# Latent heads' values as seven half-block products, and one VectorE operation on attention scores

## The chip, the cores and the metric

The kernel runs on one core of one Trainium2 chip. The metric is the device time of one execution in microseconds. Three runs of the kernel before gave 896.74, 900.17 and 900.93 us; their median is 900.17 us. An execution taken by the profiler is one more run.

## The reference

One hybrid decoder layer on 512 tokens of width 2048, in float32. Cut to what the change touches:

```python
q = (_rms_norm(q_lat, g_q) @ w_uq).reshape(b, s, 8, 192)        # 128 + 64 rotary
kv = (_rms_norm(kv_lat, g_kv) @ w_ukv).reshape(b, s, 8, 256)    # per head: 128 key, 128 value
k_nope, v = kv[..., :128], kv[..., 128:]
# latent heads: scores = (q_nope k_nope + q_rope k_rope) * 192**-0.5
# forgetting heads: scores = q k * 128**-0.5 + c[q] - c[k],  c = cumsum(log_sigmoid(f))
p = softmax(where(key <= query, scores, -inf)); o = p @ v
```

There are eight latent heads and eight forgetting heads of width 128. Their outputs, each times a SiLU gate, go through `w_out`, a norm and the residual.

## The kernel before

All large products keep float32 accuracy on TensorE by splitting each operand into a rounded part and a rest (`hi`, `lo`) and adding three matmuls (`mm3`, L148 to L151). Weights come in chunks of up to 128 x 1024. `load` (L231) starts a chunk's DMA on SP, `divide` (L269) makes `whi` with a ScalarE copy (L276) and `wlo` with a VectorE subtraction (L279). `chunk` (L289) loads four chunks ahead and divides two ahead. The raw chunks of the latent stage share three buffers.

Four of the large projections (forgetting values `v`, latents `l`, latent gates `m`, output `o`) are not multiplied plainly. They are cut in two by two half blocks and computed with seven products in place of eight, named p1, p2, p4, q6, g7, g5 and g3. `operand_steps` (L880) makes the sums of the left operand on VectorE. The sums of weight blocks (`t7`, `t6`, `t4`, `t5`) are made in DRAM by `sum_blocks` (L316): a DMA copy from SP (L312) and an accumulating DMA from POOL (L309) for each, one step at a time, paced by `paced` (L532) against the matmul loops; a step of 1 MB (the `o` sums) takes twice the pace.

The order is: forgetting heads' values, queries, keys and gates in pairs of heads (to about 460 us of the profile), latents and latent gates (to about 586 us), the latent heads in four pairs (to about 718 us), the output projection. Attention steps wait in a queue, `todo`; `pump` runs a few of them after each slice of a projection, so that their matmuls lie between those of the projection. The program order of each engine is set by a scheduler, which may move an instruction ahead of others that aren't ready in its own model.

In the latent stage each pair of heads runs a query projection (L1505: six slices of nine 512-wide matmuls), the rotary turn of the queries (L865, L870, L1514), then one loop over four slices of `w_ukv` (L1533 to L1549) that makes keys (two outputs, six 512-wide matmuls a slice) and values (four token blocks, twelve 256-wide matmuls a slice, named `mv`). PSUM has four banks for projections (`pj`), three for attention (`at`) and one for the output of a head.

`Head.scores` (L616) does, for each block of 128 queries: the score matmuls (L628); on VectorE for a latent head the mask on the diagonal block (L630) and the row maximum (L643), for a forgetting head one or two additions of `c` (L636, L639) and the maximum; on ScalarE the exponential (L650); on VectorE the reciprocal (L651) and the scaling (L652). The score bank is held until the exponential has read it. `forget_cols` (L784) turns `c` into columns with four transposes (L787); `load_keys` and `forget_keys` (L790, L795) bring `-c` rows with and without the mask. `rotary_key` (L1103) turns the shared rotary key early in the kernel.

Of the kernel before, what the change touches and what calls it, by code (L numbers as in the profile page):

```python
# [19 lines left out]
P = 128  # L20
D = 2048
S = 512
# [22 lines left out]
KL = L4 + ROPE  # L45
NSLOT = 28
# [19 lines left out]
def tile_hybrid_layer(  # L66
# [105 lines left out]
    gains2 = cst.tile([P, P], F32, name="gains2")  # L172
    pool.memset(gains2, 0.0)
# [22 lines left out]
    mask = cst.tile([P, P], F32, name="mask")  # L196
# [21 lines left out]
    raws, ready = {}, {}  # L218
# [12 lines left out]
    def load(i, small=None):  # L231
# [3 lines left out]
        if cols is None:  # L235

            raw = raw_tile(i)
            to = raw if len(w.shape) == 2 else raw.rearrange("p (k c) -> p k c", k=2)
            nc.sync.dma_start(to, w)
# [76 lines left out]
    def sum_blocks(g, block, late, width=512):  # L316

        n = 2 * width
        for name in ("t7", "t6", "t4", "t5"):

            W[name, g] = [dr.tile([P, n + 16], F32, name=f"{name}{g}{j}")[:, :n] for j in range(4)]
        for j in range(4):
# [11 lines left out]
    def add_products(names, plain):  # L334
# [3 lines left out]
        for name, g in names:  # L338
# [3 lines left out]
            else:  # L342
                for j in range(4):
                    w = W[sums[name], g][j]
                    w, second = w if isinstance(w, tuple) else (w, None)
                    of = g if g in AT else "o"
# [14 lines left out]
    for g in "vlm":  # L361
        sum_blocks(g, lambda j, h, c, g=g: in_block(g, j, h, c), ("t4", "t5"))

# [21 lines left out]
    mla = []  # L385
    for p in range(4):
        mla.append(
            {
                "q": add_chunks(
                    w_uq,  # L390
                    [
                        (0, 2 * QK * p, NOPE),
                        (NOPE, 2 * QK * p + QK, NOPE),
                        (2 * NOPE, 2 * QK * p + NOPE, ROPE),
                        (2 * NOPE + ROPE, 2 * QK * p + QK + NOPE, ROPE),
                    ],
                    QR // P, 2, 2 * QK,
                ),
                "kv": add_chunks(w_ukv, [(0, 512 * p, 512)], KVR // P, 2, 512),
            }  # L400
        )
# [141 lines left out]
    def proj_T(rng, outs, kh, kl, rate=1):  # L543
# [3 lines left out]
        for i in rng:  # L547
            hi, lo = chunk(i)
# [59 lines left out]
    class Head:  # L608
# [7 lines left out]
        def scores(self, b):  # L616
# [7 lines left out]
            else:  # L624
                for kind, (qh, ql), (kh, kl) in zip(("nope", "rope"), self.q, self.k):
                    pairs += [(qh, kh), (qh, kl), (ql, kh)] if kind == "nope" else [(qh, kh), (ql, kh)]
# [1164 lines left out]
```

## Time and profile before

| | |
|---|---|
| Median of three runs | 900.17 us (896.74 to 900.93) |
| The profiled execution, its own time | 897.76 us |
| Its span, first to last instruction | 896.0 us |
| TensorE busy | 883.9 us, 99% of the span |
| VectorE busy | 678.7 us, 76% |
| ScalarE busy | 453.8 us, 51% |
| Mean granted TensorE clock | 0.997 of 2.4 GHz |

The profile is one execution. A busy time is the union of an engine's instructions; matmuls overlap, and their ends are modelled, so the time a matmul costs is read from the distance between starts. A queue such as SP or POOL issues DMAs in order.

### The profile page before, as it was taken

To read this page: it belongs to the slowest core of one execution; us is meant where nothing else is said; L and a number is where in the kernel's file an instruction comes from. 1 tells how busy PE (TensorE), PEld (TensorE's weight loads), DVE (VectorE), ACT (ScalarE), POOL (GpSimd) and SP (SyncE) were. 2 spreads that over 40 slices of the span, in tenths; PEclk is the share of its full clock that TensorE was granted. 3 is DMA by queue.
4 is the path that set the end of the run, shared out by engine and by line. 5 is a ranking of instruction groups with operands and counts; after the bars stand their busy time and mean duration, and the time that the engine had idled before them with its cause. 6 is when DMAs were issued, how large, how long until landed. Compare 5 with 4: busy or idle time off the path is not lost.

```text
span 896.0 us, 12851 instructions
## 1 busy us (share of the span) xinstructions
PE 883.9 (99%) x4598; PEld 755.2 (84%) x4598; DVE 678.7 (76%) x1123; ACT 453.8 (51%) x837; POOL 65.7 (7%) x86
## 2 busy tenths in 40 slices
PE   9999999999999999999999999999999999999996
PEld 8988887888888888888998998788888888888885
DVE  4579995648766838577588898967877995988785
ACT  6944443334344323335445565535555676646383
POOL 1010110011211101000000000000000000000021
PEclk9999999999999999999999999999999999999998
DMA  9798799789899999996899984799762137799878
GB/s 294 235 265 250 215 322 298 233 237 305 242 278 274 245 235 254 243 267 154 275 395 393 342 297 138 159 235 233 190 147 91 51 118 219 239 325 312 269 217 250
DMA packets 125659, 218.26 MB, mean 244 GB/s; under 512 B 16378, under 2 KB 54036, under 8 KB 124572
## 3 DMA queue, kind: packets, MB, share of 16 engines
q1 hardware_dynamic: 113484, 179.47, 61.2%
q0 software_dynamic: 11376, 37.75, 20.7%
q8 instruction: 36, 0.59, 0.3%
q10 hardware_dynamic: 736, 0.22, 0.1%
q14 instruction: 27, 0.22, 0.1%
HBM read 202.72 MB, written 65.03 MB: 299 GB/s over the span
## 4 chain that ended last, share of the span: by engine, by line
PE 85%; DVE 8%; DMA 3%; ACT 2%; issue 1%; SPq 0%; DVEq 0%; ACTq 0%
PE fk L149 3%; PE fk L151 3%; PE fq L149 3%; PE fk L150 3%; PE fq L151 3%; PE fq L150 3%; PE in L585 3%; PE sm L628 2%; DVE wlo L279 2%; PE fg L149 2%; PE fg L150 2%; PE fg L151 2%; PE oa L149 2%; PE oa L151 2%; PE oa L150 2%; PE mq L149 2%
## 5 line engine op out<-in xcount | busy, mean ns | idle before, releaser
L279 DVE TENSOR_TENSOR wlo<-raw,whi 128x1024 fp32r<-128x1024 f32 (+3 forms) x217 | 256.7, 1187 | 128.2 <-ACT whi L276 125.6
L276 ACT CAST whi<-raw 128x1024 fp32r<-128x1024 f32 (+3 forms) x217 | 221.1, 1023 | 259.3 <-PE fk L150 34.1
L149 PE MATMUL fk<-h,whi 128*128 128x512 f32 x128 | 52.5, 410 | 0.0
L149 PE MATMUL fq<-h,whi 128*128 128x512 f32 x128 | 50.8, 397 | 0.0
L149 PE MATMUL fg<-h,whi 128*128 128x512 f32 x128 | 50.3, 393 | 0.0
L151 PE MATMUL fk<-h,wlo 128*128 128x512 f32 x128 | 50.2, 393 | 0.0
L150 PE MATMUL fk<-h,whi 128*128 128x512 f32 x128 | 50.1, 391 | 0.0
L151 PE MATMUL fq<-h,wlo 128*128 128x512 f32 x128 | 50.0, 390 | 0.0
L150 PE MATMUL fq<-h,whi 128*128 128x512 f32 x128 | 49.9, 390 | 0.0
L151 PE MATMUL fg<-h,wlo 128*128 128x512 f32 x128 | 49.9, 390 | 0.0
L150 PE MATMUL fg<-h,whi 128*128 128x512 f32 x128 | 49.9, 390 | 0.0
L266 DVE TENSOR_TENSOR raw<-raw,second 128x1024 f32<-128x1024 f32 x32 | 39.0, 1218 | 0.3 <-DMA second<-in_w_out_dram 0.3
L650 ACT ACTIVATE pf<-sf,stf 128x128 f32<-128x128 f32 (+3 forms) x32 | 16.7, 524 | 33.4 <-DVE stf L643 33.4
L585 PE MATMUL in<-whi,h 128*128 128x328 f32 x128 | 29.9, 321 | 0.3 <-ACT h L143 0.3
L149 PE MATMUL mq<-ln,whi 128*128 128x512 f32 x72 | 28.8, 400 | 0.0
L151 PEld LDWEIGHTS fk<-h,wlo 128*128 128x128 f32 x128 | 24.0, 188 | 5.4
L151 PEld LDWEIGHTS fq<-h,wlo 128*128 128x128 f32 x128 | 24.0, 188 | 5.3
L151 PEld LDWEIGHTS fg<-h,wlo 128*128 128x128 f32 x128 | 24.0, 188 | 5.1
L150 PE MATMUL mq<-ln,whi 128*128 128x512 f32 x72 | 28.3, 393 | 0.0
L151 PE MATMUL mq<-ln,wlo 128*128 128x512 f32 x72 | 28.2, 391 | 0.0
L149 PEld LDWEIGHTS fg<-h,whi 128*128 128x128 f32 x128 | 24.1, 188 | 4.7
L150 PEld LDWEIGHTS fg<-h,whi 128*128 128x128 f32 x128 | 24.1, 188 | 4.7
(566 smaller groups left out, 2467.1 us busy)
## 6 DMA issues: line engine op xcount, KB each, us to landing
raw<-in_w_in_dram SPq DMA_DIRECT2D x96, 512.0 KB
raw<-in_w_out_dram SPq DMA_DIRECT2D x32, 512.0 KB
second<-in_w_in_dram SPq DMA_DIRECT2D x24, 512.0 KB
bmg<-awaymg SPq DMA_DIRECT2D x20, 256.0 KB
awaymg<-rmg POOLq DMA_DIRECT2D x8, 512.0 KB, 7.5
raw<-t6v SPq DMA_DIRECT2D x8, 512.0 KB
t7o<-in_w_out_dram SPq DMA_DIRECT2D x4, 1024.0 KB
t7o<-in_w_out_dram POOLq DMA_DIRECT2D x4, 1024.0 KB, 10.2
```

Source lines behind the costliest of these rows:

```text
L149: pe.matmul(o, ah, bh, start=first, stop=False, **kw)
L150: pe.matmul(o, ah, bl, start=False, stop=False, **kw)
L151: pe.matmul(o, al, bh, start=False, stop=last, **kw)
L266: tc.keep_in_program_order(dve.tensor_tensor(out=raw, in0=raw, in1=second, op=ALU.add))
L276: cast = act.copy(hi[:, :m], raw[:, :m])
L279: dve.tensor_tensor(out=lo[:, :m], in0=raw[:, :m], in1=hi[:, :m].bitcast(F32), op=ALU.subtract)
L585: pe.matmul(banks[t][:, :n], a[k][:, tss[t]], b[:, j, :], start=k == 0 and m == 0, stop=k == NK - 1 and m == 2,)
L628: pe.matmul(s[:, :nn], a[:, qs], c[:, :nn], start=(i == 0), stop=(i == len(pairs) - 1))
L650: act.activation(p, s[:, :n], AF.Exp, bias=st[:, 0:1], scale=unit, accum_out=st[:, 1:2])
```

## The change

Four things change.

- **Values of the latent heads.** The value columns of `w_ukv` (512 x 1024) become one seven-product scheme `u` over all eight heads, with one 128 x 1024 chunk per product: twelve 512-wide matmuls each. p1 runs in the first pair before its keys; p2, q6, p4, g7 after them, with that pair's scores pumped between; g5 and g3 in the second pair. The key loop takes the key columns alone, one chunk of four slices per pair. The left operand's sums (eight steps) join `todo`; the results are combined in five slots and split per pair of heads. Four more sums of weight blocks enter the list of background steps, between those of `m` and `o`; each DMA of such a block is cut in two, and its rows are 512-byte pieces.
- **Loads.** Five of the seven chunks get tiles from the slots in place of the three shared buffers, and the loops of the latent stage load six chunks ahead.
- **Scores.** One `tensor_tensor_reduce` on VectorE adds a row mask (latent) or `c` with its mask (forgetting), negates, writes to SBUF and gives the extreme; the exponential works on SBUF in place. The term `c[q]`, the same for a whole row, is dropped, and with it `forget_cols`. Rows of `c` are loaded one and a half times per head, without the negation.
- **Rotary parts.** The rounded part and the rest of a rotary query share one tile of 128 rows, and the key is held to match (`krh`, `krl`); the number of score matmuls stays. `rotary_key` moves from the start of the kernel to the last gate projection of the forgetting heads.

The diff, cut to its core:

```diff
+        if i in up_chunks:
+            return slot(f"raw{i}", shape=(P, 1024))
...
+    def alike(to, w):
+
+        if len(w.shape) == 4:
+            to = to.rearrange("p (k h x) -> p k h x", k=2, h=4)
+            return [(to[:, k], w[:, k]) for k in range(2)]
+        return [(to if len(w.shape) == 2 else to.rearrange("p (k c) -> p k c", k=2), w)]
...
             to, _, second = bg[n - 1]
-            pool.dma_start(to.rearrange("p (k c) -> p k c", k=2), second, accum_op=ALU.add)
+            for a, b in alike(to, second):
+                pool.dma_start(a, b, accum_op=ALU.add)
         if 0 <= n < len(bg):
             to, first, _ = bg[n]
-            nc.sync.dma_start(to.rearrange("p (k c) -> p k c", k=2), first)
+            for a, b in alike(to, first):
+                nc.sync.dma_start(a, b)
...
+    def up_block(h, c):
+        rows = w_ukv[0, 2 * P * h : 2 * P * (h + 1), :]
+        return rows.rearrange("(k p) (h x) -> p k h x", p=P, x=NOPE + DV)[:, :, 4 * c : 4 * c + 4, NOPE:]
+
+    sum_blocks("u", lambda j, h, c: up_block(h, c), (), nj=1)
+    SEVEN = [(n, "u") for n in ("p1", "p2", "p4", "q6", "g7", "g5", "g3")]
+
+    def plain_up(g, h, c):
+        chunks.append((up_block(h, c), None, None, 2, 512))
...
+    mla = [{} for _ in range(4)]
+    for n in ("q0", "p1", "k0", "p2", "q6", "p4", "g7", "q1", "g5", "k1", "g3", "q2", "k2", "q3", "k3"):
+        if (n, "u") in SEVEN:
+            add_products([(n, "u")], plain_up)
+            if n not in ("p1", "p4"):
+                up_chunks.update(prods[n, "u"])
+            continue
+        p = int(n[1])
+        if n[0] == "q":
+            mla[p]["q"] = add_chunks(
...
+            mla[p]["k"] = add_chunks(
+                w_ukv, [(0, 512 * p, NOPE), (NOPE, 512 * p + NOPE + DV, NOPE)], KVR // P, 4, 2 * NOPE
+            )
...
-            hi, lo = chunk(i)
+            hi, lo = chunk(i, ahead_load)
...
+            st = pp.tile([P, 3], F32, tag="st", name=f"st{self.name}{b}", bufs=4)
+            p = pp.tile([P, n], F32, tag=f"p{b}", name=f"p{self.name}{b}")
+            to, src, row = p, s[:, :n], rows_mask[:, S - n :]
+            if self.fox is not None:
+                row = self.fox[b]
+                if len(row.shape) == 3:
+                    to, src = (a.rearrange("p (b c) -> p b c", c=P) for a in (to, src))
+
+            dve.tensor_tensor_reduce(
+                out=to, in0=src, in1=row, scale=-1.0, scalar=-NEG, op0=ALU.add, op1=ALU.min,
+                accum_out=st[:, 0:1],
+            )
+            unit = -1.0
             if self.fox is None:
-                dve.tensor_tensor(out=s[:, qs], in0=s[:, qs], in1=mask, op=ALU.add)
-            else:
-                nk, nkm, h = self.fox
-                cq = ccol[:, b, h : h + 1]
-                if b:
-                    m = b * P
-                    dve.scalar_tensor_tensor(
-                        out=s[:, :m], in0=s[:, :m], scalar=cq, in1=nk[:, :m], op0=ALU.add, op1=ALU.add
-                    )
-                dve.scalar_tensor_tensor(
-                    out=s[:, qs], in0=s[:, qs], scalar=cq, in1=nkm[:, qs], op0=ALU.add, op1=ALU.add
-                )
-            st = pp.tile([P, 3], F32, tag="st", name=f"st{self.name}{b}", bufs=4)
-            dve.tensor_reduce(out=st[:, 0:1], in_=s[:, :n], op=ALU.max, axis=AX.X, negate=True)
-            p = pp.tile([P, n], F32, tag=f"p{b}", name=f"p{self.name}{b}")
-            unit = 1.0
-            if self.fox is None:
-
-                unit = qcol[:, b : b + 1]
-                act.mul(st[:, 0:1], st[:, 0:1], unit)
-            act.activation(p, s[:, :n], AF.Exp, bias=st[:, 0:1], scale=unit, accum_out=st[:, 1:2])
+
+                unit = nqcol[:, b : b + 1]
+                act.mul(st[:, 0:1], st[:, 0:1], qcol[:, b : b + 1])
+            act.activation(p, p, AF.Exp, bias=st[:, 0:1], scale=unit, accum_out=st[:, 1:2])
...
-    def forget_cols():
-        pt = att_bank("ccol")
-        for t in range(NT):
-            pe.transpose(pt[:, t * P : (t + 1) * P], rf[:, t * P : (t + 1) * P], ident)
-        dve.tensor_copy(ccol, pt.rearrange("p (t c) -> p t c", t=NT)[:, :, R])
-
-    def load_keys(h):
+    def load_keys(h, wholes):
         both = slot(f"nk{h}")
         nc.sync.dma_start(both[:, 0, :], c_dram[h : h + 1, :].to_broadcast([P, S]))
-        return both, h
-
-    def forget_keys(both, h):
-
-        nk, nkm = both[:, 0, :], both[:, 1, :]
-        in_order(dve.tensor_scalar(out=nk, in0=nk, scalar1=-1.0, scalar2=None, op0=ALU.mult))
-        for b in range(NT):
-            c = slice(b * P, (b + 1) * P)
-            dve.tensor_tensor(out=nkm[:, c], in0=nk[:, c], in1=mask, op=ALU.add)
-        return nk, nkm, h
+        nc.sync.dma_start(both[:, 1, :HALF], c_dram[h : h + 1, :HALF].to_broadcast([P, HALF]))
+        return both, wholes[:, 1, h % 2 * P : (h % 2 + 1) * P]
+
+    def forget_keys(both, first):
+
+        full, less = (both[:, i, :].rearrange("p (b c) -> p b c", b=NT) for i in range(2))
+        for to, src in ((first, 0), (less[:, 3, :], 1), (less[:, 2, :], 2), (full[:, 3, :], 3)):
+            in_order(dve.tensor_tensor(out=to, in0=full[:, src, :], in1=mask, op=ALU.add))
+        return first, less[:, 0::3, :], both[:, 1, : 3 * P], both[:, 0, :]
...
+        k = a[:ROPE, :]
+        both = slot("kr", F32R)
+        krh, krl = (both[:, i, :] for i in range(2))
+        keys_turned.extend((krh, krl))
+        act.copy(krh[:ROPE, :], k)
+        act.copy(krw[:ROPE, :], k[:, :P])
+        hi = krh[:ROPE, :].bitcast(F32)
+        for half in range(2):
+            dve.tensor_tensor(
+                out=krl[half * ROPE : (half + 1) * ROPE, :], in0=k, in1=hi, op=ALU.subtract
+            )
+        dve.tensor_copy(krh[ROPE:, :], hi)
+        dve.tensor_copy(krw[ROPE:, :], k[:, :P])
...
+    todo.extend(operand_steps("u", 0, (raws_of[4], raws_of[0]), ("sums",), tmp, part_slot))
...
+    def up_product(name, parts, o, first):
+
+        (i,) = prods[name, "u"]
+        hi, lo = chunk(i, ahead_load=6)
+        for j in range(2):
+            for t in range(2):
+                mm3(o[t], *parts(j, t), hi[:, j, :], lo[:, j, :], first and j == 0, j == 1, skip_group_check=True)
+            pump(2)
+            paced(hi)
...
+        dve.tensor_tensor(out=a, in0=a, in1=b, op=ALU.add)
+        turned = slot(f"rq{p}", F32R)
         for i in range(2):
-            r = tmp(f"rq{p}{i}")
-            src = slice(ROPE * i, ROPE * (i + 1))
-            for half in range(2):
-                dve.tensor_tensor(
-                    out=r[ROPE * half : ROPE * (half + 1), :], in0=a[src, :], in1=b[src, :], op=ALU.add
-                )
-            q[i].append(split(r, f"rq{p}{i}", first=P))
-            qw[i].append(whole_block(wholes, 4 + i, r))
+            r = turned[:, i, :]
+            hi, lo = (slice(ROPE * h, ROPE * (h + 1)) for h in (i, 1 - i))
+            split_into(r[hi, :], r[lo, :], a[hi, :])
+            q[i].append((r, None))
+            qw[i].append(r.bitcast(F32))
...
+    def mla_k(p, wholes):
+
+        kb = [proj_bank(f"mk{p}{i}") for i in range(2)]
...
+    def mla_values(p):
+
+        c = slice(256 * (p % 2), 256 * (p % 2 + 1))
+        parts = [up[t // 2, p // 2][:, t % 2, c] for t in range(NT)]
+        values_into(v_pair(f"mv{p}"), slice(0, 256), parts)
+        for h, v in zip(heads, values_of(f"mv{p}")):
+            h.v = v
+        enqueue_values(heads)
...
+            A = two_of(proj_bank, "uA")
+            up_product("p1", latent_x(0, 0), A, True)
+            p1 = slot("up1")
+            for t in range(2):
+                act.copy(p1[:, t, :], A[t])
+            p1 = halves(p1)
+        elif p == 1:
+            G = two_of(proj_bank, "uG")
+            up_product("g5", operand("g5", "u"), G, True)
+            sub(up[1, 1], G, halves(up[1, 1]), ALU.add)
...
-                for t in range(NT):
-                    o = vb[t // 2][:, (t % 2) * 256 : (t % 2) * 256 + 256]
-                    ts = slice(t * P, (t + 1) * P)
-                    mm3(
-                        o, knh[kk][:, ts], knl[kk][:, ts], v_cols(hi, j), v_cols(lo, j),
-                        fst and t % 2 == 0, lst, skip_group_check=True,
-                    )
...
+            up_product("p2", latent_x(1, 0), A, False)
+            up[0, 0] = slot("u11")
+            for t in range(2):
+                act.copy(up[0, 0][:, t, :], A[t])
+            C = two_of(proj_bank, "uC")
+            up_product("q6", operand("q6", "u"), C, True)
+            up[0, 1] = slot("u12")
+            sub(up[0, 1], C, p1)
+            B = two_of(proj_bank, "uB")
+            up_product("p4", latent_x(1, 2), B, True)
+            up[1, 0] = slot("u21")
+            sub(up[1, 0], B, p1, ALU.add)
+            up_product("g7", operand("g7", "u"), C, False)
+            sub(up[1, 0], halves(up[1, 0]), C)
+            up[1, 1] = slot("u22")
+            sub(up[1, 1], C, p1)
+            drain()
+        elif p == 1:
+            up_product("g3", operand("g3", "u"), G, False)
+            sub(up[0, 1], G, halves(up[0, 1]), ALU.add)
+        mla_values(p)
```

## Rows read from the trace of the kernel before

**Rows 1.** The page: span, TensorE's busy share, granted clock over 40 slices.
```profile
span 896.0 us, 12851 instructions
...
PE 883.9 (99%) x4598; PEld 755.2 (84%) x4598; DVE 678.7 (76%) x1123; ACT 453.8 (51%) x837; POOL 65.7 (7%) x86
...
PEclk9999999999999999999999999999999999999998
```

**Rows 2.** The page: the chain that ended last, shares by engine.
```profile
PE 85%; DVE 8%; DMA 3%; ACT 2%; issue 1%; SPq 0%; DVEq 0%; ACTq 0%
```

**Rows 3.** Windows: length, busy (x) PE, PEld, DVE, ACT, POOL, clock, DMA share, GB/s.
```profile
400.00:460.00 60.00, 59.91 (x391) 54.72 (x390) 42.57 (x68) 29.68 (x50) 3.23 (x5) 1.00 0.80 260
593.00:612.00 19.00, 19.00 (x107) 16.47 (x106) 14.22 (x22) 7.52 (x17) 0.81 (x1) 1.00 0.98 222
612.00:646.00 34.00, 33.60 (x192) 29.33 (x191) 28.14 (x61) 19.55 (x51) 2.01 (x2) 1.00 0.85 200
682.00:718.00 36.00, 36.00 (x208) 31.25 (x206) 29.91 (x64) 23.45 (x58) 0.00 (x0) 1.00 0.19 60
```

**Rows 4.** TensorE waits for other engines, 574 to 760 us: total, times, longest.
```profile
PE oa L149 <- ACT mw L126: 0.6, 1, 0.6
PE sm L628 <- ACT pm L650: 0.4, 1, 0.4
```

**Rows 5.** Groups by form: the value matmuls, first of three like lines (L149 to L151).
```profile
L149 PE MATMUL mv<-whi,ln 128*128 128x256 f32 x64 | 18.1, 284 | 0.0
```

**Rows 6.** TensorE in order of time: start, length; twelve mv and their neighbours.
```profile
605.76 0.40 PE L149 MATMUL mk<-ln,whi 128*128 128x512 f32 x1
...
607.14 0.28 PE L149 MATMUL mv<-whi,ln 128*128 128x256 f32 x1
...
608.58 0.40 PE L149 MATMUL mk<-ln,whi 128*128 128x512 f32 x1
```

**Rows 7.** TensorE in order of time: twenty 512-wide matmuls of the output projection.
```profile
787.65 0.39 PE L149 MATMUL oc<-whi,boq 128*128 128x512 f32 x1
...
792.18 0.39 PE L151 MATMUL oc<-whi,boq 128*128 128x512 f32 x1
```

**Rows 8.** The forget columns' transposes: length, first and last start.
```profile
L787 PE MATMUL ccol<-ident,rf x4: 271/272/273, 195.9 to 196.3; 128*128 128x128 f32 x4
```

**Rows 9.** VectorE groups, 574 to 760 us: busy, mean ns, idle before.
```profile
L643 DVE TENSOR_REDUCE stm<-sm 128x1 f32<-128x128 f32 (+3 forms) x32 | 15.2, 484 | 0.4
L652 DVE TENSOR_SCALAR pm<-pm,stm 128x128 f32<-128x128 f32 (+3 forms) x32 | 12.2, 384 | 0.7
L870 DVE SCALAR_TENSOR_TENSOR rbq<-mq,sinT 32x512 f32<-32x512 f32 x16 | 11.0, 687 | 0.3
L630 DVE TENSOR_TENSOR sm<-sm,mask 128x128 f32<-128x128 f32 x32 | 9.0, 293 | 3.6 <-PE sm L628 3.2
L139 DVE TENSOR_TENSOR mk<-mk,mk 128x512 fp32r<-128x512 f32 x8 | 5.4, 690 | 0.9 <-ACT mk L138 0.9
L651 DVE RECIPROCAL stm<-stm 128x1 f32<-128x1 f32 x32 | 5.2, 162 | 8.0 <-ACT pm L650 7.6
```

**Rows 10.** VectorE groups by form, same stretch: the chunk subtractions.
```profile
L279 DVE TENSOR_TENSOR wlo<-raw,whi 128x1024 fp32r<-128x1024 f32 x23 | 28.1, 1221 | 15.3 <-ACT whi L276 14.2 <-PE sm L628 1.0
L279 DVE TENSOR_TENSOR wlo<-raw,whi 128x768 fp32r<-128x768 f32 x12 | 11.4, 954 | 3.5 <-ACT whi L276 3.4
```

**Rows 11.** ScalarE groups by form, same stretch: reading out an accumulated sum.
```profile
L650 ACT ACTIVATION_READ_ACCUMULATOR pm<-sm,stm,qcol 128x1 f32 x32 | 6.1, 192 | 0.0
```

**Rows 12.** The chain in order of time, 560 to 720 us: start, length, what.
```profile
608.25 9.60 DMA raw<-in_w_ukv_dram
617.95 1.06 ACT whi L276
...
621.90 0.86 PE sm L628 x5
```

**Rows 13.** DMA issues: KB each, median us from issue to landing.
```profile
t7o<-in_w_out_dram POOLq DMA_DIRECT2D x4, 1024.0 KB, 10.2
```

More of the change, by code (lines that the diff above doesn't have):

```diff
@@ L45 @@
 KL = L4 + ROPE
+HALF = S // 2
 NSLOT = 28
@@ L195, in tile_hybrid_layer @@
     make_identity(nc, ident)
-    mask = cst.tile([P, P], F32, name="mask")
+    rows_mask = cst.tile([P, S], F32, name="mask")
+    pool.memset(rows_mask[:, : S - P], 0.0)
+    mask = rows_mask[:, S - P :]
     make_causal_mask(nc, mask, mask_val=NEG)
@@ L237, in load @@
             raw = raw_tile(i)
-            to = raw if len(w.shape) == 2 else raw.rearrange("p (k c) -> p k c", k=2)
-            nc.sync.dma_start(to, w)
+            for a, b in alike(raw, w):
+                nc.sync.dma_start(a, b)
             raws[i] = raw
@@ L342, in add_products @@
             else:
-                for j in range(4):
-                    w = W[sums[name], g][j]
+                for j, w in enumerate(W[sums[name], g]):
                     w, second = w if isinstance(w, tuple) else (w, None)
-                    of = g if g in AT else "o"
+                    of = g if isinstance(g, str) else "o"
                     if (sums[name], of, j) in made:
@@ L1135, in load_v @@
     def load_v(pair, both):
-        nc.sync.dma_start(both, v_away[pair].rearrange("p (t c) -> p t c", t=NT))
+        in_order(nc.sync.dma_start(both, v_away[pair].rearrange("p (t c) -> p t c", t=NT)))
         return both
@@ L1248, in tile_hybrid_layer @@
     v_out(c21, 1, 0)
-    keys = [load_keys(6 + i) for i in range(2)]
+    keys = [load_keys(6 + i, wholes) for i in range(2)]
     seconds.clear()
@@ L1260, in tile_hybrid_layer @@
             drain()
-            keys = [load_keys(2 * (3 - p) + i) for i in range(2)]
+            keys = [load_keys(2 * (3 - p) + i, wholes) for i in range(2)]
             vt = load_v(3 - p, v_slot(3 - p))
@@ L1337, in latent_stats @@
         if j == 0:
-            dve.scalar_tensor_tensor(out=qcol, in0=y, scalar=SC_M, in1=rcol, op0=ALU.mult, op1=ALU.mult)
+            for to, scale in ((qcol, SC_M), (nqcol, -SC_M)):
+                dve.scalar_tensor_tensor(out=to, in0=y, scalar=scale, in1=rcol, op0=ALU.mult, op1=ALU.mult)
             return
@@ L1498, in tile_hybrid_layer, with sub, halves, latent_x @@
     knh, knl = zip(*(latents[i] for i in range(6, 10)))
-    for p in range(4):
-        c = mla[p]
+    def sub(to, x, y, op=ALU.subtract):
+        for t in range(2):
+            dve.tensor_tensor(out=to[:, t, :], in0=x[t], in1=y[t], op=op)
+    def halves(a):
+        return [a[:, t, :] for t in range(2)]
+    todo.extend(operand_steps("u", 0, (raws_of[4], raws_of[0]), ("sums",), tmp, part_slot))
+    def latent_x(half, tokens):
+        def parts(kk, t):
+            ts = slice((tokens + t) * P, (tokens + t + 1) * P)
+            return knh[2 * half + kk][:, ts], knl[2 * half + kk][:, ts]
+        return parts
+    def up_product(name, parts, o, first):
[6 more added lines that the diff above has]
+            paced(hi)
+    def mla_q(p):
         qb = [proj_bank(f"mq{p}{i}") for i in range(3)]
-        proj_T(c["q"], [(qb[i], P, cols(i * P)) for i in range(3)], qnh, qnl, rate=2)
+        proj_T(mla[p]["q"], [(qb[i], P, cols(i * P)) for i in range(3)], qnh, qnl, 2, 6)
         q = [[split(qb[i], f"mq{p}{i}", first=P)] for i in range(2)]
@@ L1518, in tile_hybrid_layer @@
-            qw[i].append(whole_block(wholes, 4 + i, r))
+            r = turned[:, i, :]
[3 more added lines that the diff above has]
+            qw[i].append(r.bitcast(F32))
+        return q, qw, wholes
+    def mla_k(p, wholes):
+        kb = [proj_bank(f"mk{p}{i}") for i in range(2)]
+        proj_T(mla[p]["k"], [(kb[i], P, two[i]) for i in range(2)], knh, knl, 2, 6)
+        k = [[split(kb[i], f"mk{p}{i}"), tuple(keys_turned)] for i in range(2)]
+        return k, [[whole_block(wholes, 2 + i, kb[i]), krw] for i in range(2)]
@@ L1519, in tile_hybrid_layer @@
+    def mla_values(p):
[5 more added lines that the diff above has]
+        enqueue_values(heads)
+    up = {}
+    for p in range(4):
+        q, qw, wholes = mla_q(p)
         if p == 0:
             set_pace(3)
-        if p == 2:
+            A = two_of(proj_bank, "uA")
[8 more added lines that the diff above has]
+            sub(up[1, 1], G, halves(up[1, 1]), ALU.add)
+        elif p == 2:
@@ L1564, in tile_hybrid_layer @@
         enqueue_scores(heads)
-        enqueue_values(heads)
+        if p == 0:
+            up_product("p2", latent_x(1, 0), A, False)
+            up[0, 0] = slot("u11")
+            for t in range(2):
+                act.copy(up[0, 0][:, t, :], A[t])
[16 more added lines that the diff above has]
+        mla_values(p)
     og = [[None] * 4 for _ in range(NT)]
@@ L1657, in load_xr @@
             nc.sync.dma_start(xr[t][c], x[piece(t, c)])
-    def sub(to, x, y, op=ALU.subtract):
-        for t in range(2):
-            dve.tensor_tensor(out=to[:, t, :], in0=x[t], in1=y[t], op=op)
-    def halves(a):
-        return [a[:, t, :] for t in range(2)]
     def done_with(t0, c, o, homes={}):
```

85 lines of the change are left out of this document (27 added, 58 removed).

## The prediction

> **What bounds the kernel now.** I read the page first, then windows of the latent stage, the waits of TensorE, single groups, and the order of time. The page says that TensorE is busy for 883.9 of 896.0 us at full clock [rows 1], and the chain that ended last runs through it for 85% [rows 2]. A busy share alone is weak, so I looked at the stage that changes: in the windows of the latent heads TensorE is busy for 33.6 of 34 us and 36.0 of 36 us, beside a VectorE at 28 to 30 [rows 3]. The only waits of TensorE for another engine from 574 to 760 us are 0.6 and 0.4 us [rows 4]. So a matmul saved there is saved in full, an operation saved on VectorE or ScalarE is worth nothing as long as TensorE doesn't wait for it, and the change can hardly win more than its matmuls. Near the bound stand VectorE (83% of 682 to 718 us) and the DMA engines (98% from 593 to 612 us, at 222 GB/s) [rows 3].
>
> **TensorE.** Removed: the value matmuls, 64 in each of three lines, 192 in all [rows 5]. Twelve of them go from 607.14 to 608.58 us, 0.120 us each [rows 6], so 23.0 us. Added: seven products of twelve 512-wide matmuls, 84. Six 512-wide ones of the same stage take 605.76 to 607.14 us, 0.230 each [rows 6]; twenty in a row elsewhere take 787.65 to 792.18, 0.2265 each [rows 7]. With 0.2285, the middle, 84 cost 19.2 us. The gain is 3.8 us; with the ends of the price and 0.119 to 0.120 for the narrow ones it is 3.5 to 4.0. This is seven eighths of the columns, less what narrow matmuls pay for their starts. Key and query projections and the score matmuls keep number and width. The four transposes of the forget columns, started over 0.4 us [rows 8], go: 0.4 us more. Sum: 4.2 us.
>
> By the Trainium skill, "TensorE: Matmul & The Clock Gate", section "Back-to-back issue gap", a warm isolated matmul starts N/2.4 + 2.5 ns after the one before, so 109 and 216 ns, and the products would save only 2.8 us. The rows disagree: both widths are slower here, and I keep the rows.
>
> **The wait at 621 us.** Score matmuls waited 0.4 us for an exponential that still held the score bank [rows 4, 12]. After the change VectorE's one operation frees the bank, so this one goes: 0.4 us. What is late next there is VectorE. The 0.6 us before the output projection I leave as it is.
>
> **VectorE around the scores.** For a latent head the mask (0.293) goes into the reduction (0.484 mean) [rows 9]. The fused operation is not in this trace. Its lower bound is the reduction alone, which reads the same columns, 0.484; its upper bound adds the mask again, 0.777. I take 0.484 plus a separate readout of the accumulator, for which the nearest row is ScalarE's 0.192 [rows 11]: 0.676. The Trainium skill, "VectorE: DVE Perf Modes", section "Two Vector instructions with no wait between them", counts an operation with an accumulator output as two instructions; by it the 0.676 stands, without it 0.484. For the forgetting heads more additions go, at no gain: TensorE is busy for 59.91 of 60 us from 400 to 460 us with VectorE at 42.6 [rows 3]. The same cover hides the moved rotary key: some seven operations of at most 0.69 us [rows 9], 5 us, into 17 us of free VectorE time; without cover it would cost its 5 us. The extra broadcast loads of `c`, and their issues on SP, are hidden there too.
>
> **VectorE in the first pair, where the products run.** This is the crowded place. From the last query matmul to the end of g7, TensorE has five products (60 x 0.2285 = 13.7 us), the keys (24 x 0.2285 = 5.5) and the scores of two heads (at 0.2285 per 512 columns 2.6 us each, and the two small blocks 0.2: 5.6): 24.8 us. VectorE has, from the means of [rows 9, 10]: the turn of the queries, eight operations of 0.687 (5.5); the keys' rests, two of 0.690 (1.4); four chunk subtractions of 1.221 and two of 0.954 (6.8); eight scores of 0.484 + 0.162 + 0.384 (8.2); the combinations of q6 and p4, four of 0.69 (2.8). That is 24.7 us, and 26.2 with eight readouts. So VectorE falls behind by some 1.5 us, and TensorE is held by full score banks or because g7 writes the banks that q6's combination still reads. New wait: 1.5 us. Lower bound 0 (the backlog slips into the next query loop, 54 x 0.2285 = 12.3 us of TensorE, where VectorE can catch up). Upper bound 4.7: g7 behind one chunk subtraction, q6's combination and two scores, without cover. The second pair has two products only and I give it nothing; the operand sums before (eight steps of two VectorE operations at most, under gates and queries) neither.
>
> **DMAs.** Each chunk of `u` is two issues on SP, each sum two on SP and two on POOL; keys take two issues per pair where the plain loads took two. SP issues ahead of use by four loops, so its time is hidden unless a load waits for a slot in front of others; what waits behind it are loads and the copies of background sums. Four sums of 0.5 MB push the 1 MB sums of `o` back, two of them out of the forgetting stage into the latent one. In the trace a load of this stage took 9.6 us to land [rows 12], and an accumulating 1 MB step 10.2 [rows 13]. Loads six ahead, divided two ahead, leave four loops; the shortest four (p2 to g7 with the scores) are 11.0 + 5.6 = 16.6 us. I take no wait.
>
> **Sum.** -4.2 - 0.4 + 1.5 = -3.1 us. The profiled execution took 897.76 us, 1.8 more than its span, so 894.7 for one like it. It lies 2.4 under the median of the runs shown, 900.17; against that median I forecast 897.0 us. The runs spread over 0.47%, so 0.5% (4.5 us) is about what a measurement can tell from no change; the forecast lies within.
>
> **Rivals.**
> - *Clean win.* VectorE's readouts cost less, or the scheduler puts products ahead of waiting scores, and no new wait comes; both old waits go: -4.2 - 1.0 = -5.2 us, 895.0. For it: TensorE has hardly waited in the whole stage [rows 4], and VectorE gains in every other pair (8 masks, and 2 to 3 rotary operations). Against: the crowded 25 us.
> - *VectorE bound.* The fused operation costs 0.777 and the first pair waits the full 4.7 us: +0.1 us, 900.3.
> - *DMA late, slower than before.* The first two pairs load 3.7 MB of value chunks and 1.0 of keys where 2.1 sufficed: 2.6 MB more, 12 us at 222 GB/s, and one more `o` sum of 2 MB moved, 9 us, against 5 us that the DMA engines had free from 612 to 646 us and none before [rows 3]. If half of the 16 us falls on the loads, p4's or g7's chunk lands 8 us late: -3.1 + 8 = +4.9 us, 905.1. It decides once a load takes over 16.6 us where it took 9.6. For it: the DMA share of 0.98, 512-byte pieces, and a chain that already passed through one load [rows 12]. Against: the earlier issue, and that sums on POOL follow one another, so they fall behind first.
> - *The products save nothing,* because wide matmuls lose their pace beside so much VectorE and ScalarE work: at 0.24 each they would save 2.8 us instead of 3.8. It shifts the sum by 1 us and stays inside the forecast.
>
> **How the numbers follow.** Forecast 0.43, clean win 0.33, VectorE bound 0.07, late DMA 0.17. Faster by over 0.5% is the clean win, 0.33; within is the forecast and the VectorE rival, 0.50; slower is the late DMA, 0.17. The range goes from 892.5 (the clean win against the profiled execution's 897.76) to 905.5 (the late DMA). Cases of both signs don't hold most of it; the forecast's own range, with waits of 0.5 to 3 us, is 896.0 to 898.5.
>
> **What the changed profile would show.** 84 matmuls of 512 columns on the products, 0.227 to 0.231 apart; no 256-wide `mv`; pairs three and four shorter by 5.8 us each (48 x 0.120), the first longer. In the first pair, waits of the score or product matmuls for VectorE of 0 to 3 us in total. The fused operation at 0.48 to 0.68 mean. Chunk copies on ScalarE not ended by a DMA. I would be wrong if the first pair shows waits above 4 us, if a `raw` load ends ScalarE's idle time before a product, or if the output projection waits for `o` sums made too late.

## The result

The changed kernel takes 903.09 us in the median of 12 runs (901.80 to 906.97), the kernel before 899.68 (12 runs, 896.74 to 903.13). The ratio is 1.0043, 95% interval [1.003, 1.0056]: slower by 0.4%, where 897.0 us and a gain of 3.1 us were forecast. The time lies in the range, on the wrong side of no change. The profiled execution took 902.74 us.

### The profile page after: what moved, and what is told of

It is laid out like the page before. It is cut to its first block, busy times and chain, and to the rows that moved or that the text cites. A ratio compares the mean times of both kernels' runs of the same rounds, so it can differ in the third digit from the quotient of the medians.

```text
span 900.7 us, 12696 instructions
## 1 busy us (share of the span) xinstructions
PE 883.2 (98%) x4486; PEld 749.3 (83%) x4486; DVE 659.6 (73%) x1106; ACT 462.4 (51%) x841; POOL 72.8 (8%) x92
## 2 busy tenths in 40 slices
DMA packets 139235, 225.07 MB, mean 250 GB/s; under 512 B 16898, under 2 KB 68892, under 8 KB 138148
## 4 chain that ended last, share of the span: by engine, by line
PE 85%; DVE 6%; DMA 5%; ACT 2%; issue 1%; SPq 0%; DVEq 0%; ACTq 0%
PE fq L150 3%; PE fk L150 3%; PE fk L152 3%; PE fk L151 3%; PE fq L152 3%; PE fq L151 3%; PE in L612 3%; PE fg L150 3%; PE fg L152 3%; PE fg L151 3%; PE sm L655 2%; PE oa L152 2%; PE sf L655 2%; PE oa L150 2%; PE oa L151 2%; DVE wlo L282 2%
## 5 line engine op out<-in xcount | busy, mean ns | idle before, releaser
L282 DVE TENSOR_TENSOR wlo<-raw,whi 128x1024 fp32r<-128x1024 f32 (+3 forms) x220 | 260.8, 1188 | 142.5 <-ACT whi L279 135.5
L279 ACT CAST whi<-raw 128x1024 fp32r<-128x1024 f32 (+3 forms) x220 | 224.4, 1023 | 242.5 <-PE fk L151 35.3
L151 PE MATMUL fk<-h,whi 128*128 128x512 f32 x128 | 50.1, 392 | 0.0
L151 PE MATMUL fq<-h,whi 128*128 128x512 f32 x128 | 49.9, 390 | 0.0
L151 PE MATMUL fg<-h,whi 128*128 128x512 f32 x128 | 49.8, 389 | 0.0
L673 ACT ACTIVATE pf<-pf,stf 128x128 f32<-128x128 f32 (+3 forms) x32 | 18.0, 563 | 61.5 <-DVE stf L664 61.5
L151 PE MATMUL mq<-ln,whi 128*128 128x512 f32 x72 | 28.9, 402 | 0.0
L151 PEld LDWEIGHTS fg<-h,whi 128*128 128x128 f32 x128 | 24.1, 188 | 4.8
```

The costliest lines, as they stand in the source:

```text
L151: pe.matmul(o, ah, bl, start=False, stop=False, **kw)
L279: cast = act.copy(hi[:, :m], raw[:, :m])
L282: dve.tensor_tensor(out=lo[:, :m], in0=raw[:, :m], in1=hi[:, :m].bitcast(F32), op=ALU.subtract)
L673: act.activation(p, p, AF.Exp, bias=st[:, 0:1], scale=unit, accum_out=st[:, 1:2])
```

## The profile after, beside the one before

The page of the changed kernel: span, busy share, granted clock over 40 slices, chain shares [rows 1, 2].

```profile
span 900.7 us, 12696 instructions
...
PE 883.2 (98%) x4486; PEld 749.3 (83%) x4486; DVE 659.6 (73%) x1106; ACT 462.4 (51%) x841; POOL 72.8 (8%) x92
...
PEclk9999999999999999999999999999989999999999
...
PE 85%; DVE 6%; DMA 5%; ACT 2%; issue 1%; SPq 0%; DVEq 0%; ACTq 0%
```

TensorE has 112 matmuls fewer and is busy 0.7 us less, but the span grew by 4.7 us. One slice of the clock, the 30th, has fallen to 8. So the saving was made and lost again at a place that the shares alone do not name. The windows of the latent stage do [rows 3] (the columns are those of that group):

```profile
593.00:612.00 19.00, 17.82 (x80) 13.93 (x80) 16.33 (x23) 11.13 (x20) 1.16 (x1) 1.00 1.00 248
612.00:646.00 34.00, 34.00 (x173) 28.78 (x172) 27.33 (x66) 21.59 (x54) 2.71 (x3) 1.00 0.97 246
646.00:682.00 36.00, 31.74 (x148) 26.34 (x147) 23.12 (x56) 17.37 (x43) 1.80 (x3) 0.91 0.90 207
682.00:718.00 36.00, 35.74 (x183) 29.98 (x182) 29.92 (x67) 24.16 (x58) 0.00 (x0) 1.00 0.28 92
```

The first pair (593 to 646 us), which the prediction called crowded, loses 1.2 us before 612 us (17.82 of 19.00) and nothing behind it (34.00 of 34). The large loss is in the third window, where the third pair starts: TensorE busy for 31.74 of 36 us, at a mean granted clock of 0.91. Before, nothing was lost there; this row of the kernel before was not among those shown:

```profile
646.00:682.00 36.00, 36.00 (x208) 31.53 (x207) 29.44 (x64) 20.57 (x55) 0.80 (x1) 1.00 0.55 152
```

The waits of TensorE in the changed kernel (who waited for whom: total, times, longest) [rows 4]:

```profile
PE ptm L682 <- DVE stm L664: 4.2, 1, 4.2
...
PE od L151 <- DVE wlo L282: 1.4, 3, 0.6
...
PE uA L150 <- ACT mw L127: 1.0, 1, 1.0
PE oa L152 <- DVE boa L140: 0.9, 1, 0.9
```

(`uA` are the banks of p1 and p2; `oa` and `od` are products of the output projection; `mw` is a copy that ScalarE makes of a block of the queries or keys.) One wait of 4.2 us is new: a transpose of probabilities waits for VectorE. The two engines in order of time around it, first TensorE, then VectorE (start, length, what, and in brackets the idle time before it and what ended it):

```profile
665.85 0.62 PE L655 MATMUL sm<-kr,rq 128*128 128x512 f32 x2
...
668.37 0.60 PE L682 MATMUL ptm<-ident,pm 128*128 128x128 f32 x4
673.17 0.90 PE L682 MATMUL ptm<-ident,pm 128*128 128x128 f32 x3 [4.21 <-DVE stm L664]
...
674.30 0.63 PE L151 MATMUL mq<-ln,whi 128*128 128x512 f32 x1
...
677.29 0.63 PE L152 MATMUL mq<-ln,wlo 128*128 128x512 f32 x1
```

VectorE, same columns:

```profile
664.20 0.35 DVE L675 TENSOR_SCALAR pm<-pm,stm 128x256 f32<-128x256 f32 x1
671.41 1.23 DVE L282 TENSOR_TENSOR wlo<-raw,whi 128x1024 fp32r<-128x1024 f32 x1 [6.86 <-ACT whi L279]
672.56 0.55 DVE L664 CUSTOM_DVE_ANT_0 pm<-sm,mask 128x384 f32<-128x384 f32 x1
...
673.03 0.69 DVE L664 CUSTOM_DVE_ANT_0 pm<-sm,mask 128x512 f32<-128x512 f32 x1
```

TensorE finished the last scores of the second pair at 666.5 us. VectorE was idle from 664.5 us, and yet it did not take these scores until 672.56. What stood before them in its order was the subtraction of a weight chunk (`wlo<-raw,whi`), for which it waited 6.86 us. The scores never needed this chunk. The chain of work, in order of time, says where the chunk was:

```profile
647.94 8.02 DMA t4o<-whi
...
655.98 0.56 SPq L324
...
656.59 0.61 SPq L259
...
657.25 12.99 DMA raw<-in_w_ukv_dram
...
670.34 1.05 ACT whi L279
...
671.41 1.23 DVE wlo L282
672.64 0.47 DVE pm L664
...
673.17 0.90 PE ptm L682 x3
674.08 0.43 PE mq L150
```

Read it from below. The fused score operation (line 664, `pm`) comes behind the chunk's split on VectorE (282) and ScalarE (279). The split waits for the third pair's key weights, `raw<-in_w_ukv_dram`, 12.99 us from the last of their issues to landing. They were issued only at 656.59, because on SP's queue they stood behind the copy of a background sum (line 324), and that copy waits for the sum's marker, a transfer of 16 numbers, to land: 8.02 us. Once it goes on, TensorE runs nine matmuls of 512 columns at 0.43 us each, where they took 0.23 before the wait. After 4.2 us of idleness the granted clock of this stretch (third figure from the end) is 0.50, the lower level of 1.2 GHz:

```profile
673.17:677.70 4.53, 4.53 (x12) 3.68 (x13) 2.86 (x8) 3.19 (x9) 0.00 (x0) 0.50 0.96 196
```

That is 9 x 0.20 = 1.8 us more.

The wait of `uA` in the first pair, 1.0 us, has the same figure in small. ScalarE, in order of time:

```profile
597.91 1.05 ACT L279 CAST whi<-raw 128x1024 fp32r<-128x1024 f32 x1 [2.52 <-DMA raw<-in_w_ukv_dram]
```

By its place in the order this is the first pair's key chunk, which came late too. Its subtraction ends on VectorE at 600.22 us, the queries' rest and the copy `mw` follow it there and on ScalarE, and `uA` goes on at 601.05.

The account: from the first query matmul to the first of the output projection it took 132.8 us before (585.84 to 718.59) and 135.9 after (585.13 to 721.03), +3.1; from there to the end +2.3; and the changed kernel came 0.7 us earlier to the first query. Together +4.7. This compares two single executions, 897.76 and 902.74 us; the medians lie only 3.4 us apart, because the profiled execution of the kernel before lies 1.9 us under its median.

The fused operation's own rows, 574 to 760 us [rows 9] (busy, mean ns, idle before):

```profile
L664 DVE CUSTOM_DVE_ANT_0 pm<-sm,mask 128x128 f32<-128x128 f32 (+3 forms) x32 | 15.2, 484 | 2.7 <-PE sm L655 2.7
...
L664 DVE DVE_READ_ACCUMULATOR2_ANT stm<- 128x1 f32 x32 | 2.6, 82 | 0.0
```

## The experiments

The theory after reading the trace: a background sum, pushed back into the third pair, holds SP's queue, the key chunk behind it comes late, and VectorE's order turns that into a wait for scores. Rivals: the products, the fused operation, the shared weight buffer or a lack of bandwidth ("capacity") is itself the cause. All ratios are against the kernel before on the same chip.

**Own tiles for the late keys.** The key chunks of pairs three and four get tiles of their own, as the products' have, so that their load waits for no buffer and goes ahead of the sum's copy.

```diff
             )
+            if p >= 2:
+                up_chunks.update(mla[p]["k"])
```

> The changed kernel, but the key chunks of the third and fourth pair get tiles from the slots, so the third pair's load stands ahead of the 1 MB copy of a background sum on SP and no longer waits for a shared raw buffer. Queue theory (the 4.2 us wait of TensorE at 669 us, and some 1.8 us of halved clock behind it, come from this one load being issued at 656.6 us behind the copy): both go, 6 us less than the changed kernel, a ratio to the kernel before of 0.996 to 0.999. Capacity theory (the DMA engines have too many bytes to move there, wherever a load stands): the load lands as late, ratio 1.003 to 1.006. Score theory (the fused operation and VectorE's order cause the wait): unchanged, 1.003 to 1.006.

Measured: 896.27 us, ratio 0.9964 [0.995, 0.9978]. SP's queue there, in order of time (`whi` is the marker's source, L326 the marker, L324 the copy):

```profile
648.55 0.25 SPq L326 DMA_DIRECT2D t4o<-whi  x1
648.90 1.15 SPq L259 DMA_DIRECT2D raw<-in_w_ukv_dram  x2
656.01 0.56 SPq L324 DMA_DIRECT2D t4o<-in_w_out_dram  x1
```

The key load goes out at 648.90 us, 7.7 us earlier, between the marker and the copy. The 4.2 us wait is gone, and the window from 646 to 682 us is back at 35.94 us and full clock. Both kernels move the same 225.07 MB, so the bytes alone are not the cause. One moved load turns +0.4% into -0.4%. But two things changed at once: the place in the queue and the buffer.

**The sum one chunk later.** Only the place: the tile stays shared.

```diff
             set_pace(3)
+            state["tiles"] = -1
```

> Change as it is, but the background sums are stepped one chunk later from the first latent pair on, so that on SyncE's queue the third pair's key load stands ahead of the last sum's marker and copy; its raw tile stays shared. Theory (place behind the sum): the 4.2 us wait of TensorE for the scores in the third pair goes, and with it the stretch at half clock; about 896 to 898 us, ratio 0.996 to 0.999. Rival (the shared raw buffer, released late by VectorE): the load still starts after 655 us and the wait stays over 3 us; ratio 1.002 to 1.006. Second rival (the whole gain of the own key tile came from elsewhere, VectorE's load of work): same, 1.002 to 1.006.

Measured: 896.40 us, 0.9985 [0.9967, 1.0002] (894.51 to 901.72); no wait of the scores. The key load now leaves at 652.37 us, ahead of the last marker, and ScalarE takes the chunk at 663.36 without waiting for a transfer. So removing the place behind the sum is enough, and the shared buffer alone does not make the wait. It does delay the load: here it goes out as VectorE's subtraction from an earlier chunk ends, at 652.31. In the changed kernel that subtraction ends at 653.19, so of the 7.7 us by which own tiles advance the load, an estimate from these rows gives about 3.4 to the queue and the rest to the buffer. The profile is that of the lowest of the seven times; the verdict rests on the ratio, whose interval lies apart from that of the change. With own tiles the runs lie closer together, 895.01 to 898.10.

**The split behind the scores.** Here the load stays late, and the order on ScalarE and VectorE changes: the third pair's key chunk is split after the second pair's last scores. To get there, all chunks split during the third pair's query projection are split one chunk ahead, not two.

```diff
-        proj_T(mla[p]["q"], ..., qnh, qnl, 2, 6)
+        proj_T(mla[p]["q"], ..., qnh, qnl, 2, 6, 1 if p == 2 else 2)
...
+        if i == mla[2]["k"][0]:
+            tc.keep_in_program_order(cast)
+            tc.keep_in_program_order(sub)
```

> Change as it is (shared raw tile, key load behind the sum), but the third pair's key chunk is split behind the last scores of the second pair in ScalarE's and VectorE's order, not ahead of them. Theory (the load lands about 670 us whatever, TensorE would need it 2 to 3 us after the flips that now wait for it; the engines' program order turns a late load into a wait of work that doesn't need it): the wait at the flip goes, a smaller one of 1 to 2.5 us comes at the first key matmul, the clock stays higher; ratio 0.999 to 1.002. Rival (the load is the bound wherever its split stands): the wait of about 4 us only moves to the key projection; 1.003 to 1.006.

Measured: 896.80 us, 0.9988 [0.9973, 1.0003]. The load is issued as late as in the change, as SP's queue shows in order of time (here the marker is L329, the copy L327):

```profile
647.91 0.25 SPq L329 DMA_DIRECT2D t4o<-whi  x1
655.78 0.56 SPq L327 DMA_DIRECT2D t4o<-in_w_out_dram  x1
656.39 1.15 SPq L259 DMA_DIRECT2D raw<-in_w_ukv_dram  x2
```

TensorE's first key matmul of the third pair, in its order of time:

```profile
677.59 0.48 PE L150 MATMUL mk<-ln,whi 128*128 128x512 f32 x1
```

TensorE wants the keys at 677.59 us and doesn't wait for them; the profile is that of the lowest of the twelve times, and the ratio bears it out. In the changed kernel the load landed at 670.24, and the split takes 1.05 + 1.23 us. It was late for the place of its split, not for its use: an estimate from these figures leaves some 5 us of reserve. The theory expected a wait of 1 to 2.5 us at the key matmul; there is none, so it was right on the mechanism and too cautious on the size.

**Sums on POOL's queue.** If SP's queue is the trouble, take the sums off it for the latent stage.

```diff
-                nc.sync.dma_start(a, b)
+                step_queue().dma_start(a, b)
...
-            nc.sync.dma_start(bg[n + 1][0][0:1, 0:16], mark)
+            step_queue().dma_start(bg[n + 1][0][0:1, 0:16], mark)
```

> The changed kernel, but from the latent stage on the background sums' copies and markers are issued on POOL, so SP holds weight loads alone; the bytes are the same. Queue theory: the key load goes out at about 649 us, no wait in the third pair, ratio 0.996 to 0.999. Capacity theory: loads land late all the same, TensorE still waits 3 us or more for the third pair, ratio 1.002 to 1.006. Score theory: 1.003 to 1.006.

Measured: 922.94 us, 1.0252 [1.0229, 1.0275], a clear miss. ScalarE in the first pair, one row:

```profile
620.92 1.04 ACT L279 CAST whi<-raw 128x1024 fp32r<-128x1024 f32 x1 [5.48 <-DMA t6o<-whi]
```

The marker is read out of the chunk's own `whi` tile, so the tile is not free until the marker has landed. On POOL a marker is issued behind an accumulating step, and the next chunk's split waits for the marker: a coupling that I had overlooked. The row shows one such wait; how much of the 24 us comes from it I did not settle. No expectation foresaw this, and it speaks neither for nor against the theory.

**The products alone** (old scores):

```diff
-            dve.tensor_tensor_reduce(out=to, in0=src, in1=row, ..., accum_out=st[:, 0:1])
+            dve.tensor_tensor(out=s[:, qs], in0=s[:, qs], in1=mask, op=ALU.add)
...
+            dve.tensor_reduce(out=st[:, 0:1], in_=s[:, :n], op=ALU.max, axis=AX.X, negate=True)
```

> The seven products, the loads and the rotary parts of the change, with the old operations around the scores (mask, maximum, c[q] and the forget columns). Queue theory: the late key load is there as in the changed kernel, ratio 1.003 to 1.007. Capacity theory: the same. Score theory: the wait goes, 0.996 to 0.999.

Measured: 901.56 us, 1.0022 [1.0007, 1.0037], with runs from 897.70 to 903.61, between the ranges of the theories. In the profiled execution (899.31 us, the second lowest of twelve) the key load goes out late, at 660.00 us and behind the sum's copy, but ScalarE waits only 0.32 us for it and TensorE not at all.

**The fused scores alone** (value matmuls as before, the diff the other way round):

> The one VectorE operation, the masked rows of c and the missing c[q] in the kernel before, with its plain value matmuls and its loads (the rotary key turned late and kept in a slot, for room). Queue and capacity theory: no products, no late load; four transposes and the 0.4 us wait less, -0.8 us, ratio 0.998 to 1.000. Score theory: slower than before, 1.003 or more.

Measured: 900.60 us, 1.0018 [1.0003, 1.0033], again between the two ranges. Its chain in the first pair has the same figure as the third pair of the change:

```profile
608.15 11.86 DMA raw<-in_w_ukv_dram
...
620.10 1.06 ACT whi L277
...
621.18 1.23 DVE wlo L280
622.41 0.47 DVE pm L638
```

A key load, its split on two engines, and only then the scores, for which TensorE waited 1.55 us. This load stood behind no sum: it went out as VectorE's subtraction from an earlier chunk freed a shared buffer. It is the small wait at 621 us of the kernel before [rows 4, 12], which I had put down to the score bank; there too the split stands ahead of the scores:

```profile
619.03 1.22 DVE wlo L279
620.25 0.48 DVE stm L643
```

Neither part alone gains. For the fused scores the trace shows why; for the products alone the one execution profiled shows no wait, and the late load is only the likely cause, which the next experiment bears out.

**Products, key tiles, old scores.**

```diff
             )
+            if p >= 2:
+                up_chunks.update(mla[p]["k"])
...
-            dve.tensor_tensor_reduce(...)
+            dve.tensor_tensor(...)
+            dve.tensor_reduce(...)
```

> Products, with own tiles for the third and fourth pair's keys as in the first experiment, but the old score operations (addition of the mask, reduction, turned masks, early masks). Theory (the products need VectorE's time, which the fused operation gives back; the products alone had no late key load to mend): about as the products alone, 900 to 903 us, ratio 1.001 to 1.004. Rival (the own key tile is worth the whole difference, the fused operation nothing): as the first experiment, 0.995 to 0.998.

Measured: 897.38 us, 0.9987 [0.9979, 0.9996]: between the two expectations. The tiles help the products alone as well (1.0022 to 0.9987), so the profiled execution of the products alone, which shows no wait, was a lucky one of a spread-out set. The expectation's premise that they had no late key load does not hold. Against 0.9964 with the fused operation, that operation is worth some 2 us once no key comes late, though the two come from different sets of runs and the intervals all but touch.

**Products without own tiles.**

```diff
-                up_chunks.update(prods[n, "u"])
+                up_chunks.update([])
```

> Change as it is, but without own tiles for the weights of the products: all of them use the shared raw buffers. Theory: the loads of the products of the first two pairs wait for VectorE's subtraction from a shared buffer and land late, a wait of 2 to 8 us at a product; ratio 1.006 to 1.015. Rival (six chunks ahead is early enough anyway, and the own tiles change only the order): 1.002 to 1.006 with the same 4 us wait in the third pair.

Measured: 902.76 us, 1.0041 [1.0028, 1.0053], the same as the change: the rival holds, the products' own tiles are worth nothing that can be measured (in its profiled execution the wait at the transposes is 1.9 us, and 2.0 us come at a key matmul).

**Four chunks ahead instead of six:**

```diff
-        hi, lo = chunk(i, ahead_load=6)
+        hi, lo = chunk(i, ahead_load=4)
...
```

(The same for the query and key projections.)

> Change as it is, but loads four chunks ahead in the latent stage as before the change. Theory: each load is issued two chunks (some 2 to 4 us) later, and the key loads behind sums come later still, so the wait in the third pair grows to 6 to 9 us; ratio 1.006 to 1.013. Rival (the later issue of the loads spreads the transfers and the sum no longer stands in the way): 0.997 to 1.001.

Measured: 902.99 us, 1.0045 [1.0026, 1.0065] (898.79 to 907.09). Neither range was hit: the median does not move, only the spread grows. In its profiled execution, the lowest of the nine times, the key load goes out at 655.38 us, straight behind the sum's copy at 654.77: what holds it is not its turn but the queue in front of it.

**Both mends.** Own key tiles and the sum one chunk later.

> Both mends at once: own tiles for the third and fourth pair's keys, and the sums stepped one chunk later. Theory (one late load, which either mend removes): no better than the better of the two alone, 895 to 898 us, ratio 0.996 to 0.999. Rival (each removes another wait): 892 to 894.5 us, 0.992 to 0.995.

Measured: 894.58 us (894.04 to 896.50), 0.9955 [0.9943, 0.9968], the best version of all. It lies between the two ranges; against own tiles alone (0.9964) the intervals overlap, so whether the second mend removes a further wait stays open (in the two profiled executions `uA` waits 0.8 us and `od` 1.4 with own tiles alone, no time and 0.4 with both). Its windows:

```profile
593.00:612.00 19.00, 18.81 (x85) 14.81 (x84) 16.41 (x26) 11.15 (x21) 1.16 (x1) 1.00 0.96 248
...
646.00:682.00 36.00, 35.95 (x183) 30.22 (x183) 28.62 (x65) 20.73 (x51) 2.84 (x3) 1.00 0.92 216
```

From the first query to the first output matmul it takes 128.4 us (585.51 to 713.88), 4.4 less than before.

**The first operands in order of use.** With own key tiles, then with the later sum: the four parts that the first output products need are split in order, not in reverse.

```diff
-            todo.extendleft([*divisions("a11", "o"), *divisions("a12", "o")])
+            todo.extendleft([*divisions("a12", "o")[::-1], *divisions("a11", "o")[::-1]])
```

> The first experiment's kernel (own tiles for keys), with VectorE splitting the four parts of the output projection's first operands in the order in which TensorE uses them, not in reverse. Theory (the 0.9 us wait of TensorE at the third kind of matmul of the first output product is only that reversed order): the wait goes, 0.5 to 1 us less than the first experiment, ratio 0.995 to 0.9965. Rival (VectorE is busy with the fourth pair's rotation there, so the wait moves to the next part): as the first experiment, 0.996 to 0.998.

Measured: 895.90 us, 0.9968 [0.9956, 0.998]. The second:

> The sums stepped one chunk later (shared raw tiles), and the four parts of the output projection's first operands split in the order of their use. Theory: the late key load is gone as with own tiles, and the wait of 0.9 us at the first output product too: 895 to 897 us, ratio 0.996 to 0.998. Rival (the order is worth nothing): as the kernel with the later sums alone, 0.9975 to 0.9995.

Measured: 896.23 us, 0.9979 [0.9966, 0.9993]. The wait of 0.9 us at `oa` is gone in both, but 0.5 us come back at a transpose behind it (the first kernel's row):

```profile
PE ptm L684 <- DVE plm L140: 0.5, 1, 0.5
```

The median of the first lies in the rival's range, but its interval reaches into both ranges; the second lies in both. So neither tells them apart. That VectorE is short there, and the order only picks who waits, is what the row suggests.

## Why the prediction was wrong

- **TensorE's saving: right.** The products run at the price taken: 21 steps of `uB` and `uC` take 621.03 to 625.81 us, 0.2276 each, against 0.2285. The stage of the best version is 4.4 us shorter. The forecast for it was 3.8 + 0.4, since the transposes' 0.4 us lie ahead of it; the old wait of 0.6 us, which I had left in, went too. The 0.4 us at 621 us went in the changed kernel, but not for my reason: with the fused operation alone the wait grew to 1.55 us. The 216 ns of the Trainium skill, "TensorE: Matmul & The Clock Gate", section "Back-to-back issue gap", is not reached here either.
- **VectorE in the first pair: not seen.** I added 1.5 us. No wait of scores or products for VectorE shows there, only 1.0 us of `uA` for ScalarE's copy `mw`, which stands behind a late key chunk. The fused operation was too dear in my sum: 0.484 mean, my lower bound, plus a readout of 0.082, not 0.192. By the Trainium skill, "VectorE: DVE Perf Modes", section "Two Vector instructions with no wait between them", it is two instructions; the trace agrees, but the second one costs a sixth of what the main one does, and the next operation starts beside it (below).
- **The step that failed: "Loads six ahead, divided two ahead, leave four loops; the shortest four [...] are 11.0 + 5.6 = 16.6 us. I take no wait."** It looked at the products' chunks in the first pair, and at the time between issue and use. The load that came late was the key chunk of the third pair, which has no product. Of its road I had the parts: the sums' issues on SP, and two sums pushed "out of the forgetting stage into the latent one". But I let sums "fall behind first" on POOL, and did not ask what stands behind a sum's copy on SP while that copy waits for its marker: 8.02 us, and SP issues nothing meanwhile. The load took 12.99 us after that, and even so its split would have been done some 5 us before TensorE needed it.
- **And behind it a term that the sum did not have:** what is queued behind the waiting split on VectorE. The order of VectorE's operations made a load that was early for its use late for work that didn't need it. The experiment with the split behind the scores shows it: same late load, no wait.
- **The clock was not priced.** 4.2 us of idle TensorE brought nine matmuls at a granted clock of 0.50, 1.8 us. This wait cost some 40% more than its length.
- **The rival "DMA late"** named the right family and nearly the right total (+4.9 us; the span grew by 4.7), but the wrong mechanism and place: p4's or g7's chunk in the first two pairs, through a lack of bandwidth, from 16.6 us of landing time on, where the late load took 12.99. That its total came near, and that the time fell into the range, is luck. One of my signs of error came true: a `raw` load ended ScalarE's idle time before a product (2.52 us of idle time ahead of p1), and 6.37 us of it in the third pair.
- **Where 4.7 us are.** In the stage: the products -3.8, the two old waits -0.4 and -0.6, the new wait +4.2, the clock +1.8, `uA` +1.0: +2.2 of its +3.1. The output stage: +2.3, in which `oa` waits 0.9 us for its operand, and `od` 1.4 us for weight chunks where it waited 0.3 before. That leaves 0.9 us of the stage and 0.3 of the output, and what makes `od`'s chunks later; I did not settle it. The 0.7 us gained ahead of the stage should hold the transposes' 0.4.

## What to carry to other kernels

When a change moves background transfers, follow each queue past the moved step: ask what is issued behind it while it waits, not only whether bandwidth suffices. Then ask on each engine what stands behind the operation that takes in the late data; put such an operation as late as its user allows. And price a TensorE wait with the clock that it may cost: here 1.8 us on top of 4.2.

## What was not expected of the hardware

A marker, a transfer of 16 numbers, took 8.02 us on SP's queue, and 11.17 and 10.07 us where POOL issued it (both in the chain of the kernel with sums on POOL):

```profile
592.17 11.17 DMA t7o<-whi
...
629.50 10.07 DMA t4o<-whi
```

By the Trainium skill, "DMA: Bandwidth & Descriptors", section "Anatomy of one DMA — SWDGE (gpsimd) path", the fixed cost of a DMA issued by POOL is about 2 us; POOL's two rows are at least five times that. The DMA engines were busy beside all three (share 0.95 from 647.90 to 656.00 us of the changed kernel, 0.96 and more in the other two stretches). What makes up the difference no run here separates.

The readout of VectorE's accumulator hides beside the next operation: both start at the same time (changed kernel, VectorE in order of time).

```profile
660.36 0.08 DVE L664 DVE_READ_ACCUMULATOR2_ANT stm<- 128x1 f32 x1
660.36 0.16 DVE L674 RECIPROCAL stm<-stm 128x1 f32<-128x1 f32 x1
```
